# Recurrent stage: projections in another order, and the rwkv scan's four chains in lockstep

## The chip, the cores and the metric

The kernel runs on one core of a Trainium2 chip. The metric is device time in microseconds (us): the time of one execution of the whole program. The core has TensorE (PE; its weight loads are shown apart as PEld), VectorE (DVE), ScalarE (ACT), GpSimd (POOL) and SyncE (SP, which issues the transfers). Each runs its own instructions in the order in which they were put into its queue, and they wait for each other through semaphores.

## The reference

Two blocks of two layers are computed for 512 tokens of width 1024, all in float32. The change touches one stage of one layer, in which two recurrent mixers run side by side on the same normed input `h`:

```python
p = h @ ab_w_in[j]
pa, pb = p[..., :A_IN], p[..., A_IN:]
q, f_fwd, f_bwd, i, g = jnp.split(pa, 5, axis=-1)
y_a = _hgrn2_mixer(q, f_fwd, f_bwd, i, g, ...)   # 4 heads of 128; last step: norm(o) * silu(g)
y_b = _rwkv7_mixer(pb, ...)                      # 8 heads of 64
mix = jnp.concatenate([y_a, y_b], axis=-1) @ ab_w_out[j]
...
def step(state, inp):                            # rwkv, forward and backward in time
    r_t, w_t, k_t, v_t, a_t, b_t = inp
    sa = jnp.einsum('bhvk,bhk->bhv', state, a_t)
    state = (state * w_t[:, :, None, :] + sa[..., None] * b_t[:, :, None, :]
             + v_t[..., None] * k_t[:, :, None, :])
    return state, jnp.einsum('bhvk,bhk->bhv', state, r_t)
```

## The kernel before

Every dense product is made from operands split into a high and a low part, three matmuls of 128x512 each (lines 423, 427 and 428, in `mm3`). The stage is the method `ab`. It has three parts.

**Projections.** `dense` walks over a weight matrix, 256 columns at a time, and gives each finished tile of 128 columns to a sink. The order is written out by hand: `values` (hgrn's i, for two heads), hgrn heads 0 and 1 (q, two forget gates and the output gate g: 512 columns each), 1024 columns of rwkv (two tiles `lat`, then k, r, v of pairs 0 and 1; a pair is two heads of 64), `values`, hgrn heads 2 and 3, and 896 columns (k, r, v of pairs 2 and 3, and the gate `gd`). The work on a head (`head_ops`) or a pair (`pair_ops`) is a generator in the queue WORK, which `dense` advances by one piece after each step of its loop; `drain(WORK)` finishes what is left before the next one is put in. `pair_ops` (lines 1568 to 1675) makes for each direction the factors `ar` and `bk` of every chunk of 64 tokens and stores them in device memory. `inverses(b)` turns 32x32 blocks of two pairs into inverses by 31 dependent steps, for pairs 0 and 1 on DVE, for 2 and 3 on POOL.

**Scan.** A chain is one pair in one direction. It goes through 8 chunks. `chunks(p, d)` does it; `before(i)` prepares a chunk, and the loop over `order` does what hangs on the state. By PE's work, a chunk of one chain is: s (scores, line 1987), tr (a transpose, 1990), v (1998), h and t (the two halves of a 32x32 block's inverse, 2003 and 2007), X (state into the right side, 2028), A (2034), U (new state, 2047), o (output from values, 2055) and o (output from the old state, 2058). Between them ACT and DVE move every result out of PSUM. Four chains run at a time, as generators in turn (`flow`, `lane`): pairs 0 and 1, then 2 and 3. The final order on each engine is a scheduler's, which works from the order of emission. `projections` puts dense work of `ab_w_out` in between (lines 423 to 428 with `aux<-os`).

**Tail.** `group_norm` of the pairs, the split of `yb`, and the last 256 rows of `ab_w_out`; then the next stage's norm begins.

Of the kernel before, what the change touches and what calls it, by code (L numbers as in the profile page):

```python
# [18 lines left out]
T = 512  # L19
D = 1024  # L20
# [35 lines left out]
def weight_order(stages):  # L56
# [64 lines left out]
def prep(i):  # L121
# [63 lines left out]
    for l in range(2):  # L185
# [3 lines left out]
        for t in range(3):  # L189
# [4 lines left out]
    a["ab_w_a"] = w_pack(np.concatenate([w[:, o + j * 128:o + j * 128 + 128] for j in range(4)  # L194
                                         for o in (0, 512, 1024, 2048)], axis=1))
    border = np.concatenate([np.arange(1536, 1792)] + [o + p * 128 + np.arange(128) for p in range(4)
                                                       for o in (512, 0, 1024)] + [np.arange(1792, 1920)])
    a["ab_w_b"] = w_pack(w[:, 2560:][:, border])
    a["ab_w_out"] = np.concatenate([w_pack(x) for x in np.split(i["ab_w_out_2"][0], [512, 768])])
# [83 lines left out]
class Net:  # L283
# [1208 lines left out]
    def ab(self, g, shift, gate):  # L1492
# [6 lines left out]
        with ExitStack() as st:  # L1499
# [39 lines left out]
            reset8 = resets(8, wk)  # L1539
            neg = self.small(0, "rw_neg", 16)  # L1540
# [9 lines left out]
            lora = wk.tile([128, 2, T], F32, tag="lora", name="lora")  # L1550
            lats = wk.tile([128, 2, T], F32, tag="lat", name="lat")
# [17 lines left out]
            def pair_ops(p, k, r, v):  # L1569
# [36 lines left out]
                for d in DIRS:  # L1606
# [33 lines left out]
                    bk = wk.tile([128, 8, 2, 64], F32, tag="bk", name="bk", bufs=2)  # L1640
                    ve.scalar_tensor_tensor(bk[:, :, 0], c8(ta_), -1.0 / UP, c8(en), op0=ALU.mult, op1=ALU.mult)
                    ar = wk.tile([128, 8, 2, 64], F32, tag="ar", name="ar", bufs=2)
# [11 lines left out]
                    bs = wk.tile([128, 8, 32], F32, tag="bs", name="bs", bufs=2)  # L1654
# [18 lines left out]
                if p == 1:  # L1673
                    self.later(POST, Fiber(inverses(0)))
# [82 lines left out]
            def head_ops(j, V, hd):  # L1757

                js = slice(j % 2 * 128, j % 2 * 128 + 128)
                th = wk.tile([128, T], F32, tag="kn", name="th", bufs=2)  # L1760
# [91 lines left out]
                on = wk.tile([128, T], F32, tag="en", name="on")  # L1852
                ve.scalar_tensor_tensor(on, O, self.v("hgrn_norm_g"), r, op0=ALU.mult, op1=ALU.mult)
                po.tensor_tensor(ya[j], ya[j], on, op=ALU.mult)

            def hgrn(V, j0):
                for j in (j0, j0 + 1):
                    hd = {}

                    def sink(m, ps):  # L1860
                        hd[m] = (hw if m == 3 else wk).tile([128, T], F32, tag="krvg"[m], name=f"hg{m}", bufs=1 if m == 3 else 2)
# [31 lines left out]
            def inverses_in(n):  # L1893

                if n in loaded:
                    return
# [357 lines left out]
```

## Time and profile before

| | |
|---|---|
| median of 3 runs | 3365.74 us (3360.74 to 3373.46) |
| profiled execution, its own time | 3370.5 us |
| its span, first to last instruction | 3368.7 us |
| mean granted TensorE clock | 0.974 of 2.4 GHz |
| PE busy | 3191.8 us, 95% of the span |
| DVE busy | 1923.2 us, 57% |
| ACT busy | 1478.4 us, 44% |
| POOL busy | 932.9 us, 28% |

Busy time on PE is modelled from pipelined instructions, so that a PE which is busy all the time can still be slower than it could be. Where starts are compared below, it is from one group of instructions to the next one on PE.

### The profile page before, as it was taken

Reading aid. Unit: us, or ns where it says so; the run is one execution under the profiler, and the core shown is the slowest. Engines: PE = TensorE matmul, PEld = TensorE weight load, DVE = VectorE, ACT = ScalarE, POOL = GpSimd, SP = SyncE. Lnnn points to the kernel's source line nnn. Section 1 sums busy time; section 2 is a strip of 40 time slices with the busy share of each in tenths; the row PEclk is TensorE's granted clock in tenths of the full one; section 3 lists DMA queues with packets and bytes.
Section 4 is the critical chain, followed back from the end, with each engine's and each line's share of the span. In section 5 each row is a group of like instructions: output and inputs, shape, how many; then the busy total and the mean of one; then the engine's idle time right before and its main releaser. Section 6 shows DMA issues by size and latency. Waiting matters only on the chain.

```text
span 3368.7 us, 46642 instructions
## 1 busy us (share of the span) xinstructions
PE 3191.8 (95%) x17382; PEld 2504.8 (74%) x17382; DVE 1923.2 (57%) x3416; ACT 1478.4 (44%) x2720; POOL 932.9 (28%) x1005
## 2 busy tenths in 40 slices
PE   5898999999999999989999999799899999899998
PEld 4665777787777777778888777577688887678887
DVE  8777665536444544464444668745754567874343
ACT  3665433334555655443343554433432335543232
POOL 5455003003642224104412030440223516540000
PEclk8899999999999999999999999799999999999999
DMA  6333567623343422234443242531244444132222
GB/s 215 119 125 86 165 203 235 209 94 123 128 144 116 148 95 91 79 131 141 164 145 115 75 119 76 138 76 35 85 143 158 150 153 136 57 119 93 96 94 82
DMA packets 234708, 417.40 MB, mean 124 GB/s; under 512 B 66160, under 2 KB 115568, under 8 KB 234480
## 3 DMA queue, kind: packets, MB, share of 16 engines
q1 hardware_dynamic: 217280, 383.82, 35.0%
q10 hardware_dynamic: 17200, 30.58, 3.3%
q8 instruction: 137, 2.24, 0.3%
q14 instruction: 91, 0.75, 0.1%
HBM read 378.64 MB, written 35.69 MB: 123 GB/s over the span
## 4 chain that ended last, share of the span: by engine, by line
PE 78%; DVE 8%; DMA 4%; POOL 4%; ACT 3%; issue 2%; SPq 0%; ACTq 0%; DVEq 0%; POOLq 0%
PE mm L423 21%; PE mm L427 20%; PE mm L428 20%; DMA adaw<-in_ada_w 4%; DVE nt L676 1%; PE s L1987 1%; POOL adacc L533 1%; DVE h_lo L682 1%; POOL cp L1402 1%; POOL adaw L532 1%; PE o L2055 1%; DVE wlo L401 1%; PE look L1071 1%; PE t L2028 1%; PE o L955 1%
## 5 line engine op out<-in xcount | busy, mean ns | idle before, releaser
L427 PE MATMUL mm<-h_lo,whi 128*128 128x512 f32 (+1 forms) x2280 | 891.5, 393 | 17.3 <-DVE h_lo L682 16.9
L423 PE MATMUL mm<-h_hi,whi 128*128 128x512 f32 (+1 forms) x2280 | 881.9, 396 | 24.6 <-ACT h_hi L681 9.0
L428 PE MATMUL mm<-h_hi,wlo 128*128 128x512 f32 (+1 forms) x2280 | 884.9, 391 | 0.0
L401 DVE TENSOR_TENSOR wlo<-wst,whi 128x1024 fp32r<-128x1024 f32 (+2 forms) x454 | 562.1, 1239 | 545.4 <-ACT whi L400 529.3
L400 ACT ACTIVATE whi<-wst 128x1024 fp32r<-128x1024 f32 (+2 forms) x454 | 455.5, 1004 | 640.5 <-PE mm L427 565.7
L423 PEld LDWEIGHTS mm<-h_hi,whi 128*128 128x128 f32 x2280 | 430.3, 192 | 128.7 <-ACT h_hi L681 12.0
L427 PEld LDWEIGHTS mm<-h_lo,whi 128*128 128x128 f32 x2280 | 436.6, 192 | 117.1 <-DVE h_lo L682 24.8
L428 PEld LDWEIGHTS mm<-h_hi,wlo 128*128 128x128 f32 x2280 | 435.0, 191 | 97.3 <-issue 2.4
L512 POOL TENSOR_SCALAR adacc<-adaw,cond_c 128x512 f32<-128x512 f32 x22 | 19.2, 874 | 795.8 <-DMA adaw<-in_ada_w 303.1
L533 POOL TENSOR_TENSOR adacc<-adacc,adaw 128x512 f32<-128x512 f32 x154 | 216.4, 1405 | 10.7
L532 POOL TENSOR_SCALAR adaw<-adaw,cond_c 128x512 f32<-128x512 f32 x154 | 141.7, 920 | 259.7 <-DMA adaw<-in_ada_w 237.3
L427 PE MATMUL mm<-r_lo,whi 128*128 128x512 f32 (+1 forms) x560 | 211.4, 377 | 0.0
L428 PE MATMUL mm<-r_hi,wlo 128*128 128x512 f32 (+1 forms) x560 | 211.0, 377 | 0.0
L423 PE MATMUL mm<-r_hi,whi 128*128 128x512 f32 (+1 forms) x560 | 211.0, 377 | 0.0
L535 DVE SCALAR_TENSOR_TENSOR adacc<-adaw,cond_c,adacc 128x512 f32<-128x512 f32 x154 | 123.0, 799 | 89.2 <-DMA adaw<-in_ada_w 87.2
L690 DVE SCALAR_TENSOR_TENSOR x<-mm,m,x 128x512 f32<-128x512 f32 (+1 forms) x130 | 85.4, 689 | 95.0 <-PE mm L428 94.6
L428 PEld LDWEIGHTS mm<-r_hi,wlo 128*128 128x128 f32 x560 | 105.8, 189 | 21.3
L427 PEld LDWEIGHTS mm<-r_lo,whi 128*128 128x128 f32 x560 | 105.8, 189 | 21.1 <-DVE r_lo L714 0.3
L423 PEld LDWEIGHTS mm<-r_hi,whi 128*128 128x128 f32 x560 | 105.7, 189 | 21.1
L1356 DVE SCALAR_TENSOR_TENSOR u<-mm,vec,u 128x511 f32<-128x511 f32 x44 | 33.0, 749 | 131.2 <-ACT u L1355 131.2
L1140 POOL TENSOR_TENSOR sq<-raw 128x512 f32<-128x512 f32 x48 | 59.3, 1236 | 123.8 <-ACT raw L1169 59.9
L517 ACT ACTIVATE adah<-adacc 128x512 fp32r<-128x512 f32 x44 | 27.7, 629 | 147.6 <-POOL adacc L533 105.3
(863 smaller groups left out, 5859.5 us busy)
## 6 DMA issues: line engine op xcount, KB each, us to landing
adaw<-in_ada_w SPq DMA_DIRECT2D x384, 256.0 KB, 3.1
wst<-in_mlp_w SPq DMA_DIRECT2D x128, 512.0 KB, 3.6
wst<-in_ffn_up SPq DMA_DIRECT2D x88, 512.0 KB, 3.5
wst<-in_dil_w_in SPq DMA_DIRECT2D x64, 512.0 KB, 3.5
P<-B SPq DMA_DIRECT2D x32, 512.0 KB, 4.5
wst<-in_ffn_down SPq DMA_DIRECT2D x32, 512.0 KB, 3.4
ib<-ix ACTq DMA_DIRECT2D x64, 129.0 KB, 4.9
B<-msk SPq DMA_DIRECT2D x16, 512.0 KB, 4.7
```

The costliest lines, as they stand in the source:

```text
L400: i = self.nc.scalar.activation(hi, st, AF.Copy)
L401: self.wlo = self.nc.vector.tensor_tensor(lo, st, hi.bitcast(F32), op=ALU.subtract)
L423: i = mm(out, lhsT=l[0], rhs=r[0], start=start, stop=False)
L427: mm(out, lhsT=l[0], rhs=r[1], start=False, stop=False)
L428: mm(out, lhsT=l[1], rhs=r[0], start=False, stop=stop)
L532: eng.tensor_scalar(tmp, a, w, 1.0, op0=ALU.mult, op1=ALU.mult)
L533: eng.tensor_tensor(acc, acc, tmp, op=ALU.add)
L535: eng.scalar_tensor_tensor(acc, a, w, acc, op0=ALU.mult, op1=ALU.add)
L676: nc.vector.scalar_tensor_tensor(t, half_of(self.x[k], h), g[k], r[h], op0=ALU.mult, op1=ALU.mult)
L682: nc.vector.scalar_tensor_tensor(l4, src, shift[k], h4.bitcast(F32), op0=ALU.add, op1=ALU.subtract)
L690: i = self.nc.vector.scalar_tensor_tensor(x, ps, gate[m], x, op0=ALU.mult, op1=ALU.add)
L1140: nc.gpsimd.tensor_tensor(sq, raw, raw, op=ALU.mult)
```

## The change

The order of the projections becomes: `values`, heads 0 and 1 (now without g, 384 columns each), all of rwkv's `lat` and four pairs (1792 columns), `values`, heads 2 and 3, and at the end 640 columns with the four gates g and `gd`. A gate now goes through `g_sink`, and the product with the normed head is made when both are there. `inverses(1)` starts when pair 3 is done. The first dense part of `ab_w_out` has 384 rows (heads 0 to 2) and all of it is issued before the scan; the second has 384 as well (head 3 and pairs 0 and 1).

The scan is one loop over 16 steps g (8 chunks for each of two rounds). Each step does one kind of matmul for all four chains and both heads of a pair, 8 matmuls of one shape, before the next kind. PE's order there is that of the code; the scheduler does not change it. s no longer multiplies padded zeros: it is 8 matmuls with 64 rows and 128 columns in place of 4 with 128 rows and 256 columns, and X is 8 of 64x64 in place of 4 of 128x128. PSUM holds one bank for X and A (`xq`), one for v, h, t and U (`uq`), one for tr, two for s and two for o.

```diff
-        for n in (1024, 896):
+        for name, n in (("ab_w_b", 1792), ("ab_w_g", 640)):
             out.extend([("ab_w_i", 4, 256)] * 2)
             for _ in range(2):
-                dense("ab_w_a", D, 512)
-            dense("ab_w_b", D, n)
-        for K in (512, 256, 256):
+                dense("ab_w_a", D, 384)
+            dense(name, D, n)
+        for K in (384, 384, 256):
             dense("ab_w_out", K, D)
...
-                if p == 1:
-                    self.later(POST, Fiber(inverses(0)))
+                if p % 2:
+                    self.later(POST, Fiber(inverses(p // 2)))
...
-                act(th, hd[3], AF.Exp, scale=-1.0)
-                sigmoid(th)
-                po.tensor_tensor(ya[j], th, hd[3], op=ALU.mult)
...
+            def g_sink(m, ps):
+                if m == 4:
+                    return b_sink(14, ps)
+                x = wg_[1].tile([128, T], F32, tag="gx", name="gx")
+                gates[m] = t = wg_[1].tile([128, T], F32, tag="gt", name="gt")
+                act(x, ps, AF.Copy)
+                act(t, x, AF.Exp, scale=-1.0)
+                sigmoid(t)
+                po.tensor_tensor(t, t, x, op=ALU.mult)
+                gated(m)
...
-            self.dense("ab_w_b", D, 1024, h, b_sink, mp)
+            self.dense("ab_w_b", D, 1792, h, b_sink, mp)
             hgrn(values(), 2)
-            self.dense("ab_w_b", D, 896, h, lambda m, ps: b_sink(8 + m, ps), mp)
+            self.dense("ab_w_g", D, 640, h, g_sink, mp)
...
-                yield from self.dense_one("ab_w_out", 512, D, y, sink, bank)
-                yield from self.dense_one("ab_w_out", 256, D, [self.split(t, os_, f"os{k}") for k, t in enumerate(yb[:2])], sink, bank)
...
+                yield from self.dense_one("ab_w_out", 384, D, last_ya + [self.split(t, os_, f"os{k}") for k, t in enumerate(yb[:2])],
+                                          sink, bank)
...
+            fill = self.dense_one("ab_w_out", 384, D, y, sink, bank)
             while self.queues[WORK] or self.queues[POST]:
                 self.step()
                 for _ in range(2):
                     next(fill, None)
+            for _ in fill:
...
+            xq, uq, rq, sq = (ctx.enter_context(tc.tile_pool(name=f"ab_{y}3", bufs=1, space=PSUM)) for y in "xurs")
...
+                ps = [sq.tile([128, 4, 128], F32, tag=f"s{e}", name="s") for e in range(2)]
+                for q, x, d, e in heads:
+                    mm(ps[e][:, q], lhsT=bk[own(e), q, at(g, d)], rhs=ar[own(e), q, at(g, d)].rearrange("p j t -> p (j t)"),
+                       start=True, stop=True)
+                sm = [wk.tile([128, 4, 128], F32, tag=f"sm{e}", name="sm", bufs=3) for e in range(2)]
+                for e in range(2):
+                    ve.tensor_tensor(*(t.rearrange("p (x d) f -> p x d f", x=2) for t in (sm[e], ps[e])), smask, op=ALU.mult)
+                bt = None
+                if g % 8 < 7:
+                    tr = rq.tile([128, 4, 128], F32, tag="r", name="tr")
+                    for q, x, d in CH:
+                        nc.tensor.transpose(tr[:, q], in_=bk[:, q, at(g, d)], identity=self.ident)
+                    bt = wk.tile([128, 4, 128], F32, tag="bt", name="bt", bufs=3)
+                    act(bt, tr, AF.Copy)
...
+            def from_values(g):
+                ps = uq.tile([128, 4, 64], F32, tag="u", name="v")
+                for q, x, d, e in heads:
+                    mm(ps[own(e), q], lhsT=scored[g][0][e][other(e), q, 0:64], rhs=VV[other(e), q, chunk(g, d), e],
+                       start=True, stop=True)
+                mixed[g] = wk.tile([128, 4, 64], F32, tag="xs", name="xs", bufs=3)
...
+                ps = uq.tile([128, 4, 32], F32, tag="u", name="h")
+                for q, x, d, e in heads:
+                    mm(ps[own(e), q], lhsT=scored[g][0][e][own(e), q, 0:64], rhs=NB[g // 8][own(e), d, x * 8 + chunk(g, d)],
...
+                ps = uq.tile([128, 4, 32], F32, tag="u", name="t")
+                for q, x, d, e in heads:
+                    mm(ps[own(e), q], lhsT=HI[own(e), q], rhs=tb[own(e), d, x * 8 + chunk(g, d), block(1 - d)],
...
-                        mm(X, lhsT=ar[:, b, 0].rearrange("p e t -> p (e t)"), rhs=S, start=True, stop=True)
-                        ve.tensor_tensor(xs, xs, X, op=ALU.add)
...
+                        X = xq.tile([128, 4, 64], F32, tag="x", name="X")
+                        for q, x, d, e in heads:
+                            mm(X[own(e), q], lhsT=ar[own(e), q, at(g, d), 0], rhs=S[own(e), q], start=True, stop=True)
+                        ve.tensor_tensor(xs, xs, X, op=ALU.add)
+                        for q, x, d, e in heads:
+                            mm(O[x + 2 * n][own(e), chunk(g, d)], lhsT=ar[own(e), q, at(g, d), 1], rhs=old[own(e), q],
...
+                        from_values(g + 1)
+                    A = xq.tile([128, 4, 64], F32, tag="x", name="A")
+                    for q, x, d, e in heads:
+                        mm(A[own(e), q], lhsT=TB[n][own(e), d, x * 8 + chunk(g, d)], rhs=xs[own(e), q], start=True, stop=True)
+                    vd = VV.rearrange("p (x d) c e t -> p d x c e t", x=2)
+                    for e in range(2):
+                        for d in DIRS:
+                            (act_copy, ve.tensor_copy)[e](vd[own(e), d, :, chunk(g, d), e], by_d(A)[own(e), d])
+                    if i < 7:
+                        S = wk.tile([128, 4, 64], F32, tag="S", name="S", bufs=2)
+                        if i:
...
+                        inverse_left(g + 1)
+                    if g < 14:
+                        scores(g + 2)
+                    if g == 9:
+                        next(norms[0])
+                    elif g == 10:
+                        next(norms[0])
+                    elif 11 <= g < 15:
+                        tiles(1)
...
+                        U = uq.tile([128, 4, 64], F32, tag="u", name="U")
+                        for q, x, d, e in heads:
+                            mm(U[own(e), q], lhsT=bt[:, q, e * 64:e * 64 + 64], rhs=VV[:, q, chunk(g, d), e], start=True, stop=True)
+                        for q, x, d in CH:
+                            c = chunk(g, d)
+                            w = su[x + 2 * n, d][:, c:c + 1]
+                            if i:
...
+                        mm(O[x + 2 * n][own(e), chunk(g, d)], lhsT=sm[e][:, q, 64:128], rhs=VV[:, q, chunk(g, d), e],
+                           start=d == 0 and i == 0, stop=d == 1 and i == 7)
+                    if g < 15:
+                        inverse_right(g + 1)
```

On PE, in the scan, the rows below are those of one stretch of about one and a half chunks of one chain, with other chains' work in between. A matmul's line says which kind it is. Before:

```order
L2055 MATMUL o<-vv_19212,sm 64x64
L2058 MATMUL o<-S,ar_19216 64x64 x2
L1987 MATMUL s<-ar_19215,bk 128x256
L1990 MATMUL s<-ident,bk 128x128
L2003 MATMUL s<-nb_19224,sm 64x32 x2
L1998 MATMUL s<-vv_19210,sm 64x64 x2
L2047 MATMUL t<-vv_19211,bt 64x64 x2
L2047 MATMUL t<-vv_19212,bt 64x64 x2
L2007 MATMUL s<-tb_19221,hi_18960 64x32 x2
```

Now a whole step of four chains, and the first row of the next:

```order
L2101 MATMUL X<-S,ar_19173 64x64 x8
L2104 MATMUL o<-S,ar_19173 64x64 x8
L2016 MATMUL v<-vv,sm 64x64 x8
L2110 MATMUL A<-xs,tb_19169 64x64 x8
L2025 MATMUL h<-nb_19170,sm 64x32 x8
L1999 MATMUL s<-ar_19359,bk_19360 128x128 x8
L2008 MATMUL tr<-ident,bk_19360 128x128 x4
L2135 MATMUL U<-vv,bt 64x64 x8
L2147 MATMUL o<-vv,sm 64x64 x8
L2034 MATMUL t<-tb_19169,hi 64x32 x8
```

Runs of one or two matmuls of a kind have become runs of 8, in a fixed order. DVE's order within such a step is (xs takes X in, vv copies A out, sm masks s, S takes U in, tb copies t out):

```order
L2102 TENSOR_TENSOR xs<-xs,X 128x256
L2114 COPY vv<-A 64x2x64 x2
L2003 TENSOR_TENSOR sm<-s,ab_mask 128x512 x2
L2140 SCALAR_TENSOR_TENSOR S<-U,su_15975,S 128x64
L2140 SCALAR_TENSOR_TENSOR S<-U,su_15976,S 128x64
L2140 SCALAR_TENSOR_TENSOR S<-U,su_15977,S 128x64
L2140 SCALAR_TENSOR_TENSOR S<-U,su_15978,S 128x64
L2037 COPY tb_19169<-t 128x2x32 x2
```

The second place is PE at the end of the projections. Before, what follows the last product with `h` is work of pairs 2 and 3 (lines 1574 to 1671), with a few dense rows between (`os`, from `ab_w_out`):

```order
L1835 MATMUL o<-qs,hS 128x64 x2
L1574 MATMUL s<-lat,lora 128x512
L423 MATMUL mm<-os0h,whi 128x512
L1835 MATMUL o<-qs,hS 128x64
L1580 MATMUL s<-lat,lora 128x512
L1574 MATMUL s<-lat,lora 128x512
```

Now the last product with `h` is followed by head 3's recurrence (lines 1835 and 1840), and the dense rows stand between its steps:

```order
L430 MATMUL mm<-h_hi_15840,wlo 128x512
L1840 MATMUL hU<-hv,kt 128x128 x3
L1827 MATMUL o<-hsm,hv 128x128 x4
L1835 MATMUL o<-qs,hS 128x64
L1840 MATMUL hU<-hv,kt 128x128 x2
L425 MATMUL mm<-os0h,whi 128x512
L1835 MATMUL o<-qs,hS 128x64 x2
```

The four pairs' work has moved ahead, into and behind the 1792 columns; from pair 0's first row (line 1578 of the changed kernel) to pair 3's last (line 1675) there are now 216 dense rows of 128x512 and 96 of 128x256 on PE.

## Rows read from the trace of the kernel before

**Rows 1.** Stretches: busy us (count) of PE, PEld, DVE, ACT, POOL; PEclk, DMA, GB/s.
```profile
1820.00:2118.00 298.00, 292.94 (x2036) 228.43 (x2034) 201.55 (x370) 146.29 (x241) 41.39 (x32) 0.99 0.27 89
2118.00:2177.00 59.00, 49.07 (x413) 33.37 (x413) 45.56 (x68) 32.16 (x61) 29.07 (x28) 0.74 0.53 131
2177.00:2377.00 200.00, 191.30 (x2153) 138.39 (x2151) 97.99 (x339) 71.16 (x317) 46.90 (x87) 0.97 0.24 62
2377.00:2403.00 26.00, 22.36 (x153) 16.61 (x152) 18.25 (x30) 8.49 (x16) 2.58 (x2) 1.00 0.20 65
```

**Rows 2.** PE's waits from 2178 to 2377: total us, times, longest.
```profile
PE aux L423 <- DVE x L690: 7.0, 1, 7.0
```

**Rows 3.** Timeline of PE in the scan: start, us, x counts passes.
```profile
2331.16 0.27 PE L1990 MATMUL s<-ident,bk 128*128 128x128 f32 x1
2331.37 0.25 PE L2007 MATMUL s<-tb,hi 64*64 64x32 f32 x2
...
2332.26 0.33 PE L2055 MATMUL o<-vv,sm 128*64 128x64 f32 x2
2332.52 0.33 PE L2058 MATMUL o<-S,ar 64*64 64x64 f32 x4
...
2333.93 0.70 PE L1987 MATMUL s<-ar,bk 128*128 128x256 f32 x2
2334.46 0.27 PE L1990 MATMUL s<-ident,bk 128*128 128x128 f32 x1
```

**Rows 4.** Timeline of PE: longer runs of one shape, and each run's successor.
```profile
2292.24 1.14 PE L2083 MATMUL t<-ident,gy 64*64 64x64 f32 x32
2293.20 0.29 PE L2034 MATMUL t<-xv,tb 64*64 64x64 f32 x4
...
2340.43 0.45 PE L2047 MATMUL t<-vv,bt 128*64 128x64 f32 x8
2340.82 0.30 PE L2007 MATMUL s<-tb,hi 64*64 64x32 f32 x4
...
1975.14 1.90 PE L1600 MATMUL o<-ident,v 64*64 64x64 f32 x32
1976.96 0.38 PE L423 MATMUL mm<-whi,h_hi 128*128 128x256 f32 x1
```

**Rows 5.** Groups by line and form from 2177 to 2400, DVE, then ACT.
```profile
L1994 DVE TENSOR_TENSOR sm<-s,ab_mask 128x256 f32<-128x256 f32 x64 | 26.7, 419 | 19.1 <-ACT bt L1992 15.3 <-PE s L1987 3.4
L2036 DVE COPY vv<-t 64x64 f32<-64x64 f32 x64 | 13.8, 226 | 15.6 <-ACT vv L2035 14.5
L2049 DVE SCALAR_TENSOR_TENSOR S<-t,su,S 128x64 f32<-128x64 f32 x48 | 12.8, 282 | 16.4 <-PE t L2047 15.5
...
L1992 ACT ACTIVATE bt<-s 128x128 f32<-128x128 f32 x56 | 15.3, 276 | 29.4 <-PE s L1990 28.5 <-PE t L2047 0.3
```

**Rows 6.** Groups from 1820 to 2177, DVE: the mask of 512 columns.
```profile
L1820 DVE TENSOR_TENSOR hsm<-s,h_mask 128x512 f32<-128x512 f32 x8 | 5.5, 684 | 0.0
```

**Rows 7.** Timeline of PE: dense rows at the full clock, and at the half clock.
```profile
1895.88 0.40 PE L423 MATMUL mm<-h_hi,whi 128*128 128x512 f32 x1
1896.11 0.40 PE L427 MATMUL mm<-h_lo,whi 128*128 128x512 f32 x1
...
2186.32 0.63 PE L427 MATMUL aux<-os0l,whi 128*128 128x512 f32 x1
2186.75 0.63 PE L428 MATMUL aux<-os0h,wlo 128*128 128x512 f32 x1
```

**Rows 8.** Stretch 2118 to 2177, line 423 on PE alone (427 and 428: x20 too).
```profile
2118.00:2177.00 59.00, 10.41 (x20) 4.55 (x20) 0.74 0.53 131
```

**Rows 9.** Line 1574 on PE: instructions' shortest, median, longest ns; first and last start.
```profile
L1574 PE MATMUL s<-lat,lora x16: 589/693/1219, 1952.9 to 2134.1; 64*128 64x512 f32 x16
```

**Rows 10.** Timeline of PE: last product of pair 1, line 1671.
```profile
2011.87 1.02 PE L1671 MATMUL o<-ks,mat 128*128 128x512 f32 x2
```

**Rows 11.** Timeline of DVE after the last output: the last split.
```profile
2391.59 0.69 DVE L368 TENSOR_TENSOR os1l<-yb,os1h 128x512 fp32r<-128x512 f32 x1 [0.70 <-ACT os1h L367]
```

More of the change, by code (lines that the diff above doesn't have):

```diff
@@ L1930, in ab @@
                     next(fill, None)
+            for _ in fill:
+                pass
             self.hold = None
+            fill = projections()
+            last_ya = [self.split(ya[3], os_, "os3")]
+            wg_[0].__exit__(None, None, None)
+            wa.__exit__(None, None, None)
             w1.__exit__(None, None, None)
@@ L1944, in ab @@
[L1944 to L1947 removed]
+            gp = E(tc.tile_pool(name="ab_gn", bufs=1, side="right"))
+            wg = gp.tile([128, 512], F32, name="rw_g2")
+            nc.sync.dma_start(out=wg, in_=ap["rw_g2"])
+            VV = wk.tile([128, 4, 8, 2, 64], F32, name="vv")
+            AB.append(slot(wk, 2))
             for t, nm, w in ((TB, "t", 64), (NB, "n", 32)):
                 t.append(wk.tile([128, 2, 16, w], F32, name=f"{nm}b1"))
[L1950 to L1951 removed]
@@ new lines, in ab @@
+                po.memset(t[1], 0.0)
+            smask = mk.rearrange("p (d f) -> p d f", d=2).unsqueeze(1).to_broadcast([128, 2, 2, 128])
+            egn = self.small(64e-5, "egn")
+            own, other = (lambda e: half_(e)), (lambda e: half_(1 - e))
+            by_d = lambda t: t.rearrange("p (x d) t -> p d x t", x=2)
+            chunk = lambda g, d: (g % 8, 7 - g % 8)[d]
+            at = lambda g, d: (g % 2, 1 - g % 2)[d]
+            heads = [(q, x, d, e) for q, x, d in CH for e in range(2)]
@@ L2103, in ab, with tiles @@
-            ended = set()
-            def lane(x):
-                flows, norm = [flow(x, d) for d in DIRS], None
+                yield
+            def tiles(n):
+                for _ in range(n * 3):
+                    next(fill, None)
+            fetch(2)
+            load_v(0, 0)
+            load_v(0, 1)
+            for x in range(2):
+                vts[x + 2] = vts[x]
+                nc.sync.dma_start(out=vts[x], in_=vsp[x + 2])
+            inverses_in(1)
+            spare = True
@@ L2108, in lane @@
                 for _ in range(2):
[L2109 removed]
+                    for y in norms:
                         next(y)
[L2111 to L2121 removed]
@@ L2122, in lane @@
-                norm = group_norm(x + 2, O[x + 2])
-                next(norm)
-                self.later(POST, Fiber(norm))
-            lanes = [lane(x) for x in range(2)]
-            for x in lanes * 2:
-                next(x)
-            self.later(POST, Fiber(inverses(1)))
-            gp = E(tc.tile_pool(name="ab_gn", bufs=1, side="right"))
-            wg = gp.tile([128, 512], F32, name="rw_g2")
-            nc.sync.dma_start(out=wg, in_=ap["rw_g2"])
-            n, spare = 0, True
-            while lanes:
-                for _ in range(1 if n < 16 or n > 48 else 0):
-                    self.hold = last["mm"]
-                    next(fill, None)
-                lanes = [x for x in lanes if next(x, self) is not self]
-                self.step()
-                n += 1
@@ L2142, in ab @@
-            self.hold = None
-            for _ in fill:
-                pass
+                tiles(3)
+                for _ in range(2):
+                    for y in norms:
+                        next(y)
+                for _ in fill:
+                    pass
             self.drain(POST)
```

294 lines of the change are left out of this document (119 added, 175 removed).

## Prediction

> **What bounds the kernel now.** The order of instructions outside the stage `ab` is the same on every engine, so I read only this stage, first by a table of stretches [rows 1]. In the 298 us of products with `h` PE is busy for 292.9 at a granted clock of 0.99. In the 59 us behind them it has the work of pairs 2 and 3 and little else: 49.1 us busy, granted clock 0.74. In the scan, 200 us, PE is busy for 191.3, DVE for 98.0, ACT for 71.2. The list of waits agrees: in the scan PE's longest wait is a single one of 7.0 us [rows 2], and 200 less 191.3 leaves hardly more for all others. So PE ends everything there, and the question is how well its 200 us are used.
>
> The timeline of PE answers that. In the scan a kind of one or two matmuls takes until the next kind starts: s 0.53 us, tr 0.21, o of two passes 0.26 [rows 3]. (A matmul in float32 is two passes.) A longer run that alternates between the two halves of the array is far cheaper: 32 passes of line 2083 take 0.96 us, 30 ns each, and eight of line 2047 take 0.39, which at 30 ns leaves 0.15 for the change of kind [rows 4]. Changes of kind and matmuls of 128 rows that run alone thus fill much of the 200 us. Third, line 1600, also 64x64 but half after half: 32 passes in 1.82, 57 ns each [rows 4].
>
> **T1, the scan.** Each step now has six kinds of 16 passes (X, o from the old state, v, A, h, t): 96 x 0.030 = 2.88 us. U and o, 16 passes each of the kind of line 2047: 2 x (0.48 + 0.07) = 1.1. s: before, two passes of 256 columns in 0.53, about 1.04 ns a column [rows 3]; now 16 of 128 columns, two at once: 1.05 (if not two at once, 2.1). tr: 0.21 for one with its change, and 0.13 for each further one (128 columns): 0.6. Sum 5.6, with the changes that are not in it 5.7.
>
> That holds if PE never waits, so I laid the step out with DVE's times: 0.42 for an operation of 256 columns, 0.23 for a copy, 0.28 for an update of S [rows 5], 0.68 for 512 columns [rows 6]; a result is there about 0.2 after the next kind could start (line 2083: 0.96 to its successor, 1.14 long [rows 4]).
> X takes 0 to 0.48, xs is added from 0.68 to 1.10. o (old) and v fill PE until 1.44, so A does not wait: 1.44 to 1.92. h wants the one bank `uq` of v, which ACT's copy frees at 2.1: to 2.6. s to 3.65. Then DVE masks two tiles, 3.85 to 5.25; PE goes on with tr (4.25), U (4.8) and o (5.35). The four updates of S stand behind the masks in DVE's queue: 5.25 to 6.4. t wants the bank of U, which they free: PE waits from 5.4 to 6.4, and the next X waits for S anyway. t ends at 6.9. **Period 6.9 us.** Behind the waiting t on PE are the next step's X, o and v; DVE has only two copies of tb left, so nothing else is late.
>
> The sum: 12 full steps of 6.9 are 83 us, less 1.7 for the steps without s and tr. The head of the scan and step 0, where two steps' s, masks and v follow each other with nothing beside them: 12.6 (1.8 periods). Steps 7 and 8, without U or without X: 10. The last one 3.2. Group norms of pairs 0 and 1, about four runs like that of line 2083 with some 2 us of waits each: 12. Four tiles of 9 dense rows put in: 36 x 0.23 [rows 7] = 8.5. At its start 13 us at the lower clock, which cost 6 (0.74 over 59 us [rows 1] is the lower level for 30 of them). Together 134 for 200: **-66**. Bounds: -93 if PE does not wait (5.7 a step, shorter ends), -43 if s does not run two at once and the changes cost 0.8 more (1.9 a step).
>
> A page speaks against the price of the runs. The Trainium skill, "TensorEngine Tiling (Array Packing)", "Restrictions and Gotchas", says that row tiles cannot access one PSUM bank at the same time, and X, v, A, h, t put both halves into one bank. The run of line 2083 writes both halves of one bank at 30 ns a pass [rows 4], so the trace disagrees. By the page the step would have the 57 ns of the third rival below.
>
> **T2, before the scan.** Before: 298 + 59 = 357 us. What is left if PE never waits: the 298; the pairs' own work of the 59 us, which is 49.1 x 0.74 = 36 us at the full clock less 60 dense rows [rows 8] at 0.23 [rows 7], so 22; 72 dense rows of `ab_w_out` that are now all issued there, 17. That is 337, or -20. The four pairs now come one after the other. Two pairs took 59 us both times, 1952.9 to 2011.9 among dense rows [rows 9, 10] and 2118 to 2177 with few; so four may need 118. PE has 216 x 0.23 + 96 x 0.12 + 2 x 22 = 105 us of work there: +13. Head 3's recurrence is now last, with 72 rows beside it: +5, an estimate (the pairs waited for 10 us in the 59). Sum **-2**, bounds -20 and +20 (all 59 us of a second two pairs' waits, twice 10, uncovered). The gates' sigmoid moves behind the recurrence and is needed only by the dense rows; inverses of pairs 2 and 3 are needed at step 8, some 60 us into the scan, and are begun earlier than before. Both I put at nothing, covered by the 72 rows and by eight steps; without that cover either would be a wait of some us once.
>
> **T3, the tail.** Before, the last split stood at 2391.6 [rows 11], 15 us after the last o, and the stretch ended at 2403 [rows 1]. Now pairs 2 and 3 end together, three dense tiles through one bank stand between the halves of the norms: **+6** (0 to +12).
>
> **Sum:** -66 - 2 + 6 = -62. The profiled execution took 3370.5 us itself; 3308.5. The median of the runs is 3365.74, 0.14% below it, so I say **3304**.
>
> **Rivals.**
> 1. The waits vanish: DVE's updates get in front of t and the pairs' waits are half of what I put. T1 -93, T2 -11, T3 +6: -98, so 3268. For it: by the times above DVE is busy for less than 4 of the 6.9 us. Against: the masks stand ahead of the updates in its queue.
> 2. The clock is at its lower level through the scan. Each step then has about 1 us in which PE waits, and in the trace the granted clock was 0.74 in the one stretch where PE waited repeatedly. At 1.2 GHz a dense row takes 0.43 in place of 0.23 [rows 7]; 5.7 becomes 10.5 a step, with a rest of the wait 11: the scan takes 200 again. T1 0: +4, so 3370. Against: before, the scan held 0.97 with a wait of 7 us in it [rows 1, 2]. The Trainium skill, "TensorE: Matmul & The Clock Gate", "A second HAM failure mode: psum-queue depth-cycling", tells of a kernel in which frequent short idle times between groups, as PSUM banks are cycled, make the clock swing between its levels; `uq` is cycled so here. No row of before shows a PE that waits for 1 us in each 7.
> 3. The halves do not run two at once when the data come from such tiles: 57 ns a pass as line 1600 [rows 4], +2.6 a step, 15 steps: +39. Total -23, so 3343. Against: lines 2083 and 2047.
> 4. The one that ends slower: the pairs, one behind the other, starve PE in the 105 us of T2, and the clock falls to its lower level over all of it, as it did with two pairs alone (0.74 [rows 1]). Work of 105 us takes 1.85 times as long: +89, T2 +87, total +27, so 3393. For it: four generators' worth of steps in one queue, one dense step between two pieces. Against: at 1953 to 2012 two pairs among dense rows ran in the stretch with 0.99. It decides from T2 at about +60.
>
> **How the numbers follow.** Forecast 0.73, rival 1 0.10, rival 2 0.06, rival 3 0.06, rival 4 0.05. The forecast's own range is 3275 to 3340 (T1 by 20, T2 by 20, T3 by 6, not all one way). The range 3255 to 3350 takes in rivals 1 and 3 and leaves out 2 and 4 and a little more. A measurement of this kernel can tell about 0.5%, 17 us, from no change. Faster: forecast, rivals 1 and 3, 0.88; within 0.5%: rival 2 and a rest of the forecast, 0.07; slower: 0.05.
>
> **What would show it.** In the scan, a step from X to X of about 6.9 us; PE's one regular wait before t, for DVE's update of S (line 2140), some 1 us; s's run 1.05, a run of 16 passes 0.48; granted clock near 1; the scan about 134 us, with its first row about 2175 to 2180 and a tail of 32 us. Runs of 0.9 would be rival 3, a granted clock of 0.5 to 0.7 in the scan rival 2, a start of the scan after 2230 rival 4. What would make me wrong: a wait between engines that I did not lay out (ACT's two copies of HI and four of S in one queue, 0.2 to 0.3 each), or a PE that spends more between kinds than 0.15 us.

## The result, and the profile after

The changed kernel takes 3315.25 us (median of 4 runs, 3311.48 to 3316.4); the kernel before took 3367.02 in the 4 runs beside it. The ratio is 0.9839, with a 95% interval of 0.9824 to 0.9854: faster by 1.6%, 52 us. The forecast was 3304 us, with a range of 3255 to 3350. The profiled execution took 3315.12 us itself, 55 less than that of before.

The table of stretches after, cut where the work ends that [rows 1] shows for before (busy us of PE, PEld, DVE, ACT, POOL with counts; granted clock; DMA):

```profile
1820.00:2110.00 290.00, 283.65 (x2122) 217.25 (x2122) 201.76 (x380) 154.50 (x259) 49.80 (x54) 0.99 0.35 106
2110.00:2184.00 74.00, 60.41 (x349) 45.95 (x347) 42.40 (x63) 26.84 (x49) 49.17 (x66) 0.86 0.40 98
2184.00:2202.00 18.00, 7.93 (x97) 6.75 (x98) 10.44 (x19) 5.60 (x15) 2.98 (x2) 0.59 0.84 169
2202.00:2249.00 47.00, 42.12 (x1036) 37.93 (x1034) 23.55 (x77) 18.04 (x66) 3.16 (x8) 0.94 0.26 78
2249.00:2317.50 68.50, 60.22 (x1230) 51.33 (x1227) 38.91 (x105) 23.99 (x82) 3.17 (x8) 0.95 0.12 33
2317.50:2351.00 33.50, 25.61 (x163) 19.14 (x161) 19.49 (x30) 9.43 (x18) 2.77 (x3) 0.95 0.17 55
```

Ahead of the scan there are now 290 + 74 = 364 us where there were 357; the scan takes 18 + 47 + 68.5 = 133.5 in place of 200; the tail 33.5 in place of 26. So the whole gain lies in the scan, -66.5, and some 14 us of it are given back around it.

One step of the scan on PE (timeline; x counts passes, the bracket is idle time ahead of a row and what ended it); it answers to [rows 3, 4]:

```profile
2215.06 0.66 PE L2034 MATMUL t<-tb,hi 64*64 64x32 f32 x16 [0.59 <-DVE S L2140]
2215.52 0.69 PE L2101 MATMUL X<-S,ar 64*64 64x64 f32 x16
2216.01 0.49 PE L2104 MATMUL o<-S,ar 64*64 64x64 f32 x10
2216.28 0.27 PE L2016 MATMUL v<-vv,sm 64*64 64x64 f32 x2
2216.30 0.28 PE L2104 MATMUL o<-S,ar 64*64 64x64 f32 x3
...
2217.45 0.66 PE L2025 MATMUL h<-nb,sm 64*64 64x32 f32 x16
2218.03 1.16 PE L1999 MATMUL s<-ar,bk 64*128 64x128 f32 x16
2219.13 0.66 PE L2008 MATMUL tr<-ident,bk 128*128 128x128 f32 x4
2219.71 0.69 PE L2135 MATMUL U<-vv,bt 128*64 128x64 f32 x16
2220.23 0.64 PE L2147 MATMUL o<-vv,sm 128*64 128x64 f32 x16
2221.45 0.65 PE L2034 MATMUL t<-tb,hi 64*64 64x32 f32 x16 [0.59 <-DVE S L2140]
```

From one t to the next are 6.39 us. X takes 0.49 to its successor (31 ns a pass), s 1.10, tr 0.58, U 0.52: the prices of the forecast. The one wait stands where it was laid out, ahead of t, but it is 0.59 us and not 1.0. Rows of o and v stand between each other because each half of the array goes through its own matmuls: the first half is at v while the second is still at o.

DVE in the same step:

```profile
2216.24 0.42 DVE L2102 TENSOR_TENSOR xs<-xs,X 128x256 f32<-128x256 f32 x1
...
2219.23 1.29 DVE L2003 TENSOR_TENSOR sm<-s,ab_mask 128x512 f32<-128x512 f32 x2 [0.82 <-PE s L1999]
2220.45 0.86 DVE L2140 SCALAR_TENSOR_TENSOR S<-U,su,S 128x64 f32<-128x64 f32 x4
```

The two masks take 1.22 us from their start to the updates, and the four updates 0.86. The forecast had 1.37 and 1.13 from the mean of one [rows 5, 6]; back to back, an instruction begins 0.07 to 0.09 us before the row of the one ahead ends.

PE's waits, first from 2193 to 2318 (to be held against [rows 2]), then from 2095 to 2202, those over 4 us:

```profile
PE v L2016 <- DVE sm L2003: 9.0, 1, 9.0
PE t L2034 <- DVE S L2140: 8.4, 12, 1.2
...
PE mm L425 <- ACT gx L1868: 6.1, 1, 6.1
PE mm L425 <- DVE x L692: 4.7, 1, 4.7
```

The waits of the step add up to 8.4 us. The other three were not laid out. Behind them stand one engine and one queue, as the timeline of POOL, ACT, DVE and SP's queue shows:

```profile
2104.06 0.91 POOL L1692 TENSOR_TENSOR inv_t<-inv 128x31 f32<-128x31 f32 x1 [66.50 <-DMA inv<-in_eye]
...
2127.78 0.73 POOL L1694 TENSOR_TENSOR inv<-inv,inv_t 128x256 f32<-128x256 f32 x1
2128.47 1.26 POOL L1871 TENSOR_TENSOR gt<-gt,gx 128x512 f32<-128x512 f32 x1
...
2129.76 0.60 ACT L1868 ACTIVATE gx<-mm 128x512 f32<-128x512 f32 x1 [12.05 <-POOL gt L1871]
2129.76 1.11 DVE L1861 TENSOR_TENSOR ya<-ya,gt 128x512 f32<-128x512 f32 x1 [9.18 <-POOL gt L1871]
...
2162.53 0.52 SPq L1703 DMA_DIRECT2D tinv<-inv  x1
2163.14 3.37 SPq L392 DMA_DIRECT2D wst<-in_ab_w_out  x2
...
2173.10 1.79 ACT L402 ACTIVATE whi<-wst 128x768 fp32r<-128x768 f32 x2 [15.72 <-DMA wst<-in_ab_w_out]
```

The inverses of pairs 2 and 3 begin on POOL at 2104, as pair 3 is done. The product of the first gate, for which ACT was done at 2117, comes behind 24 us of them; ACT, DVE and then PE stand still for it. Later two stores of finished inverses (lines 1703 and 1704, issued from 2161.96) stand in SP's queue ahead of loads of `ab_w_out`. Issued at 2163.14, these loads are there at 2173.1, 10 us later; in e9, with no store ahead of them, the same two take 5.4 (2149.94 to 2155.3). The last dense tiles wait for these weights: their split on DVE holds up the residual that frees the bank, so that the wait is put down to line 692. The two stores took 1.1 us of SP's time; that the rest of the delay is their bytes ahead of those of the weights was not tried apart.

### The profile page after: what moved, and what is told of

Read it like the earlier page. It is cut to its first block, busy times and chain, and to the rows that moved or that the text cites. A ratio compares the mean times of both kernels' runs of the same rounds, so it can differ in the third digit from the quotient of the medians.

```text
span 3313.3 us, 46673 instructions
## 1 busy us (share of the span) xinstructions
PE 3111.3 (94%) x17622; PEld 2462.9 (74%) x17622; DVE 1896.6 (57%) x3282; ACT 1457.6 (44%) x2570; POOL 921.4 (28%) x995
## 4 chain that ended last, share of the span: by engine, by line
PE 73%; DVE 9%; DMA 6%; POOL 5%; ACT 3%; issue 3%; SPq 1%; ACTq 0%; DVEq 0%; POOLq 0%
PE mm L425 20%; PE mm L429 20%; PE mm L430 20%; DMA adaw<-in_ada_w 4%; DVE nt L678 1%; POOL adacc L535 1%; DVE wlo L403 1%; DVE h_lo L684 1%; POOL cp L1404 1%; ACT whi L402 1%; POOL adaw L534 1%; DVE acc L1400 1%; DVE adacc L537 1%; PE o L1303 1%; PE s L1999 1%
## 5 line engine op out<-in xcount | busy, mean ns | idle before, releaser
L370 DVE TENSOR_TENSOR ssl<-sq,ssh 128x512 fp32r<-128x512 f32 x48 | 40.5, 843 | 93.0 <-ACT ssh L369 90.4
```

The lines of the kernel that those rows point to most:

```text
L370: (sub or nc.vector).tensor_tensor(lo, src, hi.bitcast(F32), op=ALU.subtract)
```

## The experiments

All edits are to the changed kernel, except e4. Stretches from the profiles: from the stage's first normed tile to the last dense row ahead of the scan (before: to 2177), from there to the last o, and from there to the next stage's first normed tile; and the time from X to X in the first round.

| | ahead | scan | tail | X to X | median us |
|---|---|---|---|---|---|
| before | 351 | 200 | 33 | - | 3367.0 |
| changed | 358 | 133 | 40 | 6.39 | 3315.25 |
| e1 U first | 359 | 128 | 41 | 5.89 | 3310.19 |
| e2 halves in turn | 359 | 164 | 36 | 8.15 | 3347.17 |
| e3 s and tr mixed | 358 | 152 | 44 | 7.74 | 3337.94 |
| e4 order alone | 355 | 188 | 34 | - | 3361.33 |
| e5 gates on DVE | 363 | 130 | 44 | 6.39 | 3321.52 |
| e6 values later | 359 | 133 | 36 | 6.39 | 3314.85 |
| e7 three banks | 359 | 133 | 33 | 6.39 | 3311.12 |
| e8 all four | 364 | 127 | 33 | 5.89 | 3305.93 |
| e9 inverses later | 337 | 137 | 46 | 6.39 | 3305.53 |
| e10 three edits | 338 | 132 | 34 | 5.89 | 3289.22 |

### e4: the order of the projections alone

The kernel before with the first part of the change, up to the scan; in the scan only:

```diff
-            self.later(POST, Fiber(inverses(1)))
-                for _ in range(1 if n < 16 or n > 48 else 0):
+                for _ in range(1 if n > 48 else 0):
```

> Edit: the kernel before, with the new order of the projections, the gates apart, the first 384 rows of ab_w_out all ahead of the scan and the inverses of pairs 2 and 3 begun with pair 3; the scan is the old one, chain by chain. Theory (the gain of 52 us lies in the lockstep; the order alone only moves work): the stretch ahead of the scan is about 7 us longer and holds 12 more dense rows, the scan has 36 dense rows (8 us) less in its first part and no work of inverses on POOL; the sum is near 0, a median of 3355 to 3370 us. Rival (the order itself brings a good part): 3345 us or less.

3361.33 us, ratio 0.9981 (0.9972 to 0.9991): 6 us of the 52. Ahead of the scan it is 4 us longer, and the old scan, with 36 dense rows (8 us) less in it, 12 us shorter. The rest, some 46 us, belongs to the lockstep, if the two parts add up. The theory holds.

### e2: the halves of the array in turn

```diff
-            heads = [(q, x, d, e) for q, x, d in CH for e in range(2)]
+            heads = [(q, x, d, e) for e in range(2) for q, x, d in CH]
```

> Edit: within each run of 8 matmuls the four of one half of the array come first, then the four of the other; same matmuls, same kinds. Theory (a run is cheap because neighbours lie in different halves and run two at once): a pass costs 57 ns in place of 30, as in the line of before that takes the halves in turn; a kind of 16 passes takes 0.9 in place of 0.5, s more, and a step 2.6 to 4.5 us longer; 15 steps make +40 to +65 us, a median of 3355 to 3380 us, most of the gain gone. Rival (the runs are cheap because they have one shape, whatever the order of halves): the step stays at 6.4 us and the median at 3315.

3347.17 us, ratio 0.9942 (0.9927 to 0.9957). 32 of the 52 us are lost by the order of matmuls within a run alone, so the rival is out: the pairs of halves are a part of the gain. But a step is 1.76 us longer, not 2.6 to 4.5. PE's timeline shows why:

```profile
2223.00 0.56 PE L2101 MATMUL X<-S,ar 64*64 64x64 f32 x10
2223.36 0.27 PE L2104 MATMUL o<-S,ar 64*64 64x64 f32 x1
2223.41 0.22 PE L2101 MATMUL X<-S,ar 64*64 64x64 f32 x1
...
2226.20 1.71 PE L1999 MATMUL s<-ar,bk 64*128 64x128 f32 x16
2227.84 0.65 PE L2008 MATMUL tr<-ident,bk 128*128 128x128 f32 x4
```

Where the next kind has the same tile shape, its first half begins while the second half of the kind ahead still runs: o stands at 2223.36 between rows of X. It ends at a change of shape: s takes 1.64 us to its successor in place of 1.10.

### e3: s and tr in turns

```diff
                 for q, x, d, e in heads:
                     mm(ps[e][:, q], lhsT=bk[own(e), q, at(g, d)], rhs=ar[own(e), q, at(g, d)].rearrange("p j t -> p (j t)"),
                        start=True, stop=True)
+                    if e and g % 8 < 7:
+                        nc.tensor.transpose(tr[:, q], in_=bk[:, q, at(g, d)], identity=self.ident)
```

> Edit: s and tr are no longer runs of 8 and of 4, but two of s, one of tr, four times over; nothing else moves. Theory (a change of tile shape costs PE 0.1 to 0.15 us): seven... six more changes a step, 0.6 to 0.9 us; the masks come as much later, so the wait behind them stays; 14 steps make +8 to +13 us, a median of 3323 to 3328 us. Rival (changes of shape cost nothing, the gain is that two matmuls of a half-array pair run at once, which this keeps): period 6.4, median 3315.

3337.94 us, ratio 0.9917 (0.9895 to 0.9938): more than the theory had, 1.35 us a step. On PE:

```profile
2222.66 0.66 PE L2035 MATMUL t<-tb,hi 64*64 64x32 f32 x16 [0.89 <-DVE S L2141]
...
2225.64 0.49 PE L2002 MATMUL s<-ar,bk 64*128 64x128 f32 x4
2226.07 0.33 PE L2005 MATMUL tr<-ident,bk 128*128 128x128 f32 x1
2226.32 0.49 PE L2002 MATMUL s<-ar,bk 64*128 64x128 f32 x4
```

Four passes of s take 0.43, where a quarter of the long run is 0.27; one tr 0.25 where a quarter of its run is 0.15. The block of s and tr grew from 1.68 us to 2.72 for six more changes: 0.17 each, above the 0.10 to 0.15 of the theory. DVE's masks come later and the wait ahead of t grows by 0.30. In the changed kernel a step has four changes of shape; chain by chain most kinds, of one or two matmuls each, were one.

### e1: U ahead of s

```diff
                     if g < 14:
-                        scores(g + 2)
+                        turned(g + 2)
...
+                    if g < 14:
+                        scores(g + 2)
                     if g == 9:
```

`turned` holds the transposes, which were a part of `scores`; the lines left out are those of U and its updates of S, moved up.

> Edit: in each step of the scan tr and U come right behind h, and s only behind U, so that DVE's updates of S stand ahead of its masks. Theory (a step is PE's own 5.8 us and a wait of 0.59 us, because the updates of S stand behind the masks in DVE's queue and t behind them in the bank of U): the wait goes, the period falls from 6.39 to about 5.8 us, in the second round too; some 13 steps make about -8 us, a median near 3307 us. Rival (another wait was hidden under it: U now comes 1.1 us earlier, and DVE's copy of vv starts only when ACT's is done): PE waits for vv ahead of U instead, the period stays at 6.3 to 6.4, median 3313 to 3317.

3310.19 us, ratio 0.9831 (0.9817 to 0.9846). The median is 5 us below the changed kernel, but the intervals overlap, so it is the profile that settles it: a step is 5.89 us in place of 6.39, and the scan 128 in place of 133. On DVE the updates now come first, and no wait is left in the full steps:

```profile
2224.46 0.86 DVE L2142 SCALAR_TENSOR_TENSOR S<-U,su,S 128x64 f32<-128x64 f32 x4 [0.93 <-PE U L2137]
...
2225.53 1.29 DVE L2003 TENSOR_TENSOR sm<-s,ab_mask 128x512 f32<-128x512 f32 x2 [0.22 <-PE s L1999]
```

The theory's wait was the right one; 5.89 is what PE needs by itself (5.7 in the forecast).

### e5: the gates' products on DVE

```diff
-                po.tensor_tensor(t, t, x, op=ALU.mult)
+                ve.tensor_tensor(t, t, x, op=ALU.mult)
```

> Edit to the changed kernel: the product of a gate with its sigmoid (line 1871) is made by DVE in place of POOL. Theory (what made the stretch ahead of the scan longer than forecast is POOL's queue: the first two gates stand behind some 24 us of the inverses of pairs 2 and 3, which now begin with pair 3; ACT waits 12 us and DVE 9.2 us for them, PE 6.1 us): PE's wait of 6.1 us goes, with 1 to 3 us of the waits behind it; the scan begins 6 to 9 us sooner, median 3306 to 3309. Rival (the end of the stretch is set by the weights of ab_w_out, for which PE waits 4.7 us later on): PE waits as much longer there, median 3313 to 3316.

3321.52 us, ratio 0.9865 (0.985 to 0.988): no gain, 6 us more. The wait for the gate is gone, and this one has grown from 4.7 us (PE's waits):

```profile
PE mm L425 <- DVE x L692: 13.3, 1, 13.3
```

The rival was right. The loads of weights are issued at 2176.9, later than in the changed kernel (2163.14), because SP's queue itself waits for POOL here: 7.6 us with the loads of `tb`, for POOL's memset of TB and copies into HI, which stand amid the inverses, and 3.0 us with a store, for an inverse. Taking one of two waits with one cause away only moved the time to the other.

### e9: the inverses later

```diff
-                if p % 2:
-                    self.later(POST, Fiber(inverses(p // 2)))
+                if p == 1:
+                    self.later(POST, Fiber(inverses(0)))
...
-                    po.tensor_copy(HI[half_(e), q, block(1 - q % 2)], self.ident[half_(e), o:o + 32])
+                    set_hi = po.tensor_copy(HI[half_(e), q, block(1 - q % 2)], self.ident[half_(e), o:o + 32])
+            self.later(POST, Fiber(inverses(1)))
```

The first product of these inverses is given an order behind `set_hi`, so that the scheduler can't place it ahead of that.

> Edit to the changed kernel: the inverses of pairs 2 and 3 stand on POOL behind the four gates, the memset of TB and the copies into HI, and so behind the last loads of ab_w_out in SP's queue, as their stores are issued later; same work, gates on POOL as in the changed kernel. Theory (what the stretch ahead of the scan lost against the forecast is the early inverses, twice: 6.1 us for gates behind them on POOL, 4.7 us for weights behind their stores on SP; taking the gates off POOL alone moved the wait to the weights, 13.3 us): both waits go, the scan begins 8 to 11 us sooner, median 3304 to 3307. Rival (the inverses are then late for step 7, which reads them: POOL needs about 57 us from there on): 5 to 10 us of it come back as a wait of PE between steps 7 and 8; median 3311 to 3316.

3305.53 us, ratio 0.9812 (0.9798 to 0.9825), 10 us below the changed kernel. Both waits are gone. POOL and SP's queue show it; the products of the first two gates begin at 2120, as soon as ACT is done, and the five loads of weights stand ahead of the stores:

```profile
2120.11 3.61 POOL L1873 TENSOR_TENSOR gt<-gt,gx 128x512 f32<-128x512 f32 x2 [79.77 <-ACT gt L1563]
...
2149.94 18.46 SPq L392 DMA_DIRECT2D wst<-in_ab_w_out  x5
2185.21 0.52 SPq L1706 DMA_DIRECT2D ninv<-inv  x1
```

The stretch ahead of the scan is 21 us shorter, more than the 8 to 11 forecast, because the waits on the way were 13.5 us together (6.1, 4.7, 1.7, 0.8 and 0.2 in the changed kernel), and without them PE also held its full clock there, 1.00 where it had been 0.88 from 2095 to 2184 (table of stretches):

```profile
2095.00:2165.00 70.00, 69.74 (x435) 54.39 (x434) 43.08 (x75) 30.48 (x53) 32.55 (x48) 1.00 0.48 129
2165.00:2186.00 21.00, 7.79 (x81) 6.38 (x81) 13.76 (x19) 6.17 (x16) 18.90 (x31) 0.61 0.40 117
```

Half of that comes back. The tail of this execution was 6 us longer (below). The second row is the scan's head, where PE's wait for the first masks has grown from 9.0 to 12.1 us, and this is a price of the move: the inverses are now on POOL beside the DVE work for which PE waits. From the last residual to the masks DVE takes 11.6 us in place of 8.4. Of these 3.1 us, 2.0 are the copies of v (8 in 6.17 us in place of 4.21) and 1.2 three operations with two inputs:

```profile
2170.86 6.17 DVE L1994 COPY vv<-vt 64x256 f32<-64x256 f32 x8
```

The last section tells how POOL does this. No wait for the inverses appeared at step 7: X to X over steps 7 and 8 is 16.3 us, as in the changed kernel.

### e6: half of the copies of v later

```diff
             load_v(0, 0)
-            load_v(0, 1)
...
                 inverse_right(0)
+                load_v(0, 1)
```

> Edit to the changed kernel: half of the copies of v (those of the chunks that are read last) are issued behind the scan's head in place of ahead of it, 4 of 8 on DVE and 4 of 8 on ACT. Theory (PE's wait of 9.0 us ahead of the first v is DVE's queue: the split of head 3, then 8 copies at 0.52 us, then the masks): the wait falls by 2.1 us to about 6.9, the copies find room later; median 3312 to 3314. Rival (they come ahead of the masks or updates of the first steps): first step longer by as much, 3315.

In this kernel and in e8 the later copies read v's tile after pairs 2 and 3 had been loaded into it, so half of the chunks of pairs 0 and 1 are computed from those values; the amount of work is the same. 3314.85 us, ratio 0.9844 (0.9829 to 0.9859): no difference. The wait fell from 9.0 to 8.2, not by 2.1. DVE's copies are not alike (timeline of the second copy, the third, and two of those that went, with POOL's two memsets):

```profile
2186.36 1.94 POOL L1977 MEMSET tb<- 128x2048 f32 x1 [24.20 <-DVE os3l L370]
2186.48 1.96 DVE L1991 COPY vv<-vt 64x256 f32<-64x256 f32 x1
2188.24 1.09 POOL L1977 MEMSET nb<- 128x1024 f32 x1
2188.37 1.11 DVE L1991 COPY vv<-vt 64x256 f32<-64x256 f32 x1
...
2194.64 0.49 DVE L1991 COPY vv<-vt 64x256 f32<-64x256 f32 x2 [3.77 <-DMA vt<-vsp]
```

A copy takes 0.28 us by itself. The second and the third begin while a memset is running on POOL, and each ends 0.14 us behind the end of its memset. The changed kernel shows the same two, of 1.96 and 1.11, among six of 0.27 to 0.28; the 0.52 of the theory is the mean of these eight. So the edit moved four cheap copies, some 0.2 each in a row, and 0.8 is just what the wait lost. The theory named the right queue and a wrong price. Some 2.5 us of the 9.0 (1.96 and 1.11 less twice 0.28) are due to the two memsets; no run moves those.

### e7: three banks in the tail

```diff
-            bank = lambda: self.aux.tile([128, T], F32, tag="aux", name="aux") if spare else mp.tile([128, T], F32, tag="mm", name="mm")
+            bank = lambda: ends.pop().tile([128, T], F32, tag=ends.pop(), name="end") if ends else self.aux.tile([128, T], F32, tag="aux", name="aux") if spare else mp.tile([128, T], F32, tag="mm", name="mm")
...
+                ends.extend(["u", uq, "x", xq, "r", rq])
                 tiles(3)
```

> Edit to the changed kernel: the three tiles of ab_w_out behind the scan are made in the scan's free banks (tr's, X's and v's) in place of one bank one after the other. Theory (the tail is longer than before because PE waits there for that bank: 3.7, 0.8 and 0.8 us, and the norms' transposes stand behind): the 27 rows take 6.4 us in a row, the transposes start when DVE's norms are ready, some 5 to 7 us sooner; median 3308 to 3310. Rival (the norms on DVE and ACT are the chain there, and the residuals come in their way): 0 to 2 us, 3313 to 3315.

3311.12 us, ratio 0.9839 (0.9822 to 0.9855). In the profile the tail is 33.2 us in place of 39.6, and the norms' transposes start 6.5 us behind the last o (13.7 in the changed kernel): the theory's size. The whole time doesn't settle it: the median is 4 us lower, the ratio to the runs beside it the same. Nor would one profile, as the tail differs between executions (last section). But the three kernels with this edit have tails of 33 to 34 us (e7, e8, e10), and the seven with the one bank (the changed kernel, e1, e2, e3, e5, e6, e9) 36 to 46.

### e8 and e10: together

e8 joins e1, e5, e6 and e7; e10 joins e1, e9 and e7.

> Edit to the changed kernel: the four edits together, U ahead of s (measured -5), gates on DVE, half of the copies of v later, and the three banks. Theory (they lie in different stretches, so they add up): -5 - 7 - 2 - 6 = -20, a median of 3293 to 3297. Rival (weights end the stretch ahead of the scan, norms the tail): the step's 5 us alone and little more, 3306 to 3311.

3305.93 us, ratio 0.9819 (0.9804 to 0.9833): -9 in place of -20. Its stretch ahead of the scan is 364 us, with a wait of 16.0 us for the weights: the rival, by the cause that e9 then removed.

> Edit to the changed kernel: U ahead of s, the inverses later, and the three banks in the tail, together. Theory (three stretches of their own): -5 - 10 - 5 = -20, a median of 3293 to 3298. Rival (the shorter first round leaves POOL less time, so that PE waits for the inverses at step 7 and the edits overlap): 3300 to 3308.

3289.22 us (5 runs, 3286.15 to 3294.41), ratio 0.9765 (0.9752 to 0.9778). That is 26 us below the changed kernel, somewhat more than forecast, and 78 below the kernel of before: the fastest version of this study.

## Why the prediction was right, and where it was off

**T1, the scan: -66 forecast, -66.5 measured, but by errors that cancel, which is luck.** The period was 6.39 and not 6.9: DVE's masks and updates were priced at the mean of single rows, and take 0.15 and 0.27 us less back to back. With that, the first round's six periods and the seven of the second (7.65 to 8.55 us with norms or dense rows in them) took 88 us; the forecast's full steps, norms and tiles add up to 102. Against it, the head with the lower clock took 25.7 us from the last dense row to the first X, and not 18.6: DVE's queue there holds the split of head 3 and eight copies of v ahead of the first masks, which I did not lay out (PE's wait of 9.0 us; e6 bears out the queue, and shows 2.5 us of it beside POOL's memsets). And steps 7 and 8 took 16.2 in place of 10, because the first norms' instructions stand on DVE ahead of the copies of t's result (a wait of 2.3) and PE ran at the lower clock behind it.

**The price of the runs held.** 31 ns a pass for X and s at 1.10 are the terms of the sum. e2 shows that the pairs of halves are needed for it, e3 that changes of shape cost 0.17 us each. The sums of PE's time from the start of each row to the next one, by kind, waits between them included, over the scans of before and after (worked out from the timelines; the first step's s and tr ran among the last dense rows and are not in it): s 34.9 to 19.1 us, X 20.1 to 6.9, tr 18.7 to 8.5, o (both) 42.9 to 26.2, U 13.1 to 8.0, v 12.2 to 8.7, A 14.9 to 11.4; h and t, which were short already, 20.9 to 21.8. How much of s and X is due to the padded zeros that are gone, and how much to runs, was not tried apart, but the columns allow an estimate. For four chains, s had 8 passes of 256 columns one after the other, 2048 columns at 1.04 ns [rows 3]; now it has 16 passes of 128, two at a time, which is the time of 1024 columns, at 1.07 ns (1.10 us). So what s gained is that two halves run at once where zeros were; its price per column is the old one. X had 8 passes of 64 columns, 512, and has now 16 of 64, two at a time, again the time of 512; yet four chains cost 1.44 us before (20.1 us for 56 matmuls) and 0.49 now. So X gained by standing in a run, and not by the zeros.

The page "TensorEngine Tiling (Array Packing)" of the Trainium skill ("Restrictions and Gotchas") says that two row tiles cannot access one PSUM bank at the same time; X, v and A run at 30 to 31 ns a pass into one bank, so this trace disagrees as line 2083 did before. Its "Key Properties" say that a change of tiling mode drains TensorE and that tiles otherwise work independently: e3's 0.17 us a change and e2's interleaved rows agree.

**T2: -2 forecast, +7 measured; this is the term that failed.** The pairs were not the trouble: from 1944.4 to 2061 they took 117 us, for 118 forecast, and PE did not starve (clock 0.99). The step that was wrong is "both I put at nothing": the gates and the inverses of pairs 2 and 3. I had the inverses begun earlier and covered, and did not ask what stands behind them on POOL (the gates: PE waits 6.1 us) and on SP, whose queue holds their stores and the loads behind them (4.7 us). e5 showed that the gate alone is not it, e9 that the inverses are: placed later, they give 21 us in that stretch and 10 in the whole time.

**T3: +6 forecast, +7 measured**, by the waits for the one bank, as laid out (e7); but with that bank the tail is 36 to 46 us long from one profile to another, so the agreement to a us is luck.

**The rivals.** 1 (no waits) did not happen, but e1 and e10 show that its step can be had: 5.89 us. 2 (the lower clock through the scan) did not: with a wait of 0.59 us in each 6.39 the granted clock was 1.00 (table of stretches, changed kernel):

```profile
2209.00:2248.00 39.00, 34.61 (x913) 31.32 (x911) 20.42 (x68) 15.27 (x56) 3.16 (x8) 1.00 0.28 84
```

So the swing that the Trainium skill tells of ("TensorE: Matmul & The Clock Gate", "A second HAM failure mode: psum-queue depth-cycling") did not show at this rate of waits. Rival 3's price is that of e2's order, at 1.76 us a step and not 2.6. Rival 4 did not happen.

## What to carry to other kernels

Where a scan of small matmuls keeps one engine busy, price a matmul by its neighbours: the same tile shape next to it, in the other half of the array. Then lay the step out engine by engine and look for the one whose queue holds something that nobody waits for (masks) ahead of something that somebody does (updates). And when work is moved earlier on an engine "with time to spare", list what stands behind it there and behind its transfers: taking away one of two waits with one cause shows nothing until the cause itself is moved. Look also at what POOL runs beside DVE's instructions for which another engine waits: here a copy of 0.28 us took 1.96.

## What the runs showed of the hardware that was not expected

**The clock in the tail differs between executions of the same instructions.** From about the last o to the next stage's norm PE has the same work and the same waits in the changed kernel and in e9, yet (table of stretches of the changed kernel, then of e9):

```profile
2316.00:2357.00 41.00, 30.22 (x190) 22.59 (x189) 26.12 (x40) 13.46 (x26) 5.94 (x5) 0.93 0.15 47
```

```profile
2301.00:2348.00 47.00, 36.17 (x190) 26.28 (x190) 26.03 (x40) 13.41 (x26) 5.87 (x5) 0.78 0.12 42
```

The granted clock was 0.93 and 0.78 and the stretch 41 and 47 us long; in e5 it was 0.85. In e10, with those waits for the bank gone, it was 0.95 in 35 us. That the waits for the bank lower it is not shown: where the longest of them was 1.1 us (e1) the clock was 0.84 in 42 us, and where it was 1.5 (e2) 1.00 in 37 us.

**An operation of DVE waits for the end of POOL's.** The product of line 1861 (512 columns, two inputs) took 0.69 us at 2186, with POOL idle, and 1.09 to 1.17 at 2129 to 2141, amid the inverses:

```profile
2133.99 1.01 POOL L1694 TENSOR_TENSOR inv<-inv,inv_t 128x252 f32<-128x252 f32 x1
2134.38 1.17 DVE L1861 TENSOR_TENSOR ya<-ya,gt 128x512 f32<-128x512 f32 x1
```

All three long ones end 0.54 to 0.55 us behind the end of the instruction of POOL that was running when they began, here 2135.55 behind 2135.00. In e9, where the inverses come later, three of the four took 0.68, and the fourth, at 2168 and amid the inverses, 1.09; it too ends 0.54 behind POOL's. So the excess of 0.4 to 0.5 us is the rest of POOL's instruction. The Trainium skill has a rule for it, "SBUF — State Buffer", "SBUF: two separate sides": DVE and GpSimd share a pair of ports, and of an operation of DVE with two inputs in SBUF and one of GpSimd that reads SBUF, the one that starts second is blocked for the whole length of the first. The rows agree.

The copies of v, with one input, are held in the same way, beside memsets too (e6: 1.96 and 1.11 us in place of 0.28, each ending 0.14 us behind POOL's memset). In e9 one copy of v takes 3.32 us: it begins while POOL works on an inverse and ends 0.15 us behind the second of the two memsets that follow. The masks, whose first input is in PSUM, take 0.67 each there, amid the inverses, as they do with POOL idle.
